# Splitting the weights of a hybrid attention block a load at a time (1,024 columns) in place of half a load

## The chip, the cores and the metric

One core of a Trainium2 chip runs the whole program. The metric is the device time of one execution in microseconds; of each kernel several executions are timed and the median is given. The profile is that of one further execution, taken by the hardware profiler.

The engines that matter: PE multiplies matrices (PEld loads its stationary operand), DVE and ACT do elementwise work, SP issues the transfers from memory (DMA). Every engine works through its own list of instructions in order and waits at one whose inputs are not ready.

## What is computed

A decoder block: a norm, one wide projection, two token mixers (sparse attention with a compressed, a selected and a sliding branch, and retention), gates, an output projection, a second norm and the residual. Cut to what matters here:

```python
h = rms_norm(x, norm_pre)                       # x: 512 tokens x 1024
proj = h @ w_in                                 # 1024 x 6936
q_n, k_c, v_c, k_s, v_s, k_w, v_w, g_n, z_n, q_r, k_r, v_r, z_r, m_a, m_b = split(proj)
kc = gelu(blocks(rope(k_c)) @ cmp_w1_k) @ cmp_w2_k        # compressed keys, values alike
o_a = g_0 * attend(q, kc, vc) + g_1 * attend(q, selected) + g_2 * attend(q, window)
y_a = (o_a * silu(z_n)) @ w_nsa_o
y_b = (group_norm(retention(q_r, k_r, v_r)) * silu(z_r)) @ w_ret_o
merged = sigmoid(m_a) * y_a + sigmoid(m_b) * y_b
y = x + rms_norm(merged @ w_out, norm_post)
```

## The kernel before

**Two halves of a number.** The matmuls take operands rounded to a shorter format (fp32r). To keep the precision of float32 each operand is split into its rounded value `hi` and the rest `lo`, and a product is three matmuls: hi by hi, hi by lo, lo by hi (`mm3`). For the weights this is done on the chip, while they stream in: a rounding (raw to `whi`, on ACT or DVE) and a subtraction (raw less `whi` to `wlo`, always on DVE).

**The weight stream.** All weights come in one order as 128-row pieces of 1024 columns, 512 KB each (`stream_shape`): load 0 in two halves, three more for the first projection, four of 560 columns (C, the keys' and values' columns), four for the queries (Q), eight for the hidden layer of the compression (H0 to H7), then blocks of four loads in the order of `PLAN` (Z, MA, ZR, QK, VR, ...; NO has two), and eight for the last projection. One load holds two *parts*: two k-tiles (128 rows of the contraction) of 512 columns each, and a matmul uses one part. In the hidden layer each part serves two steps of 256 columns, so a load is four pairs of matmuls.

**The buffers.** Raw loads lie in `NR` = 4 buffers (tile `raw`). `splitter` makes the parts in stream order. Each part takes one `whi` and one `wlo` tile of 512 columns, out of `NW` = 9 of each; the parts of C have storage of their own (`WC`). `in_ring` counts the parts without those of C. A tile comes free when the last matmul on its part has run (`used_up`, the list `done`). `split_lo` makes the subtraction; with the second part of a load it issues the next transfer (`load_next`, L315), so a raw buffer is filled again only once both its parts are split.

**The matmuls of a block.** `nat` (tokens as rows) and `tra` (transposed) run over the k-tiles for one output tile; four output tiles go through the same eight parts, and on the last of them each part is released as it is used. Then the next block's parts are wanted in the same order. `hidden` does the compression's first layer, H0 to H3 for the keys and H4 to H7 for the values.

**What sets the order.** The program is a set of generators. `Order` runs them while the kernel is built: it keeps a modelled time for PE (`now`) and for the other engines (`eng`), and always lets that generator go on which is ready by the model, by priority. `cp_any` puts a rounding on ACT or on DVE, whichever the model has done sooner (DVE has 400 ns against it). The subtraction of part p has priority 0 when p is at most `SOON` = 2 past the part that PE last asked for (`rank`), and 4 otherwise. The main line of projections has the lowest priority, 9, and attention 2 or 3. So each engine's list is fixed when the program is built, and a change of a duration or of a buffer count moves instructions on every engine.

Lines that the profile names: L222 matmul, L226 transpose on PE, L189 any ACT instruction, L197 rounding on DVE, L201 any two-input DVE instruction, L522 doubling of the keys ahead of their transposes, L315 the raw transfers. From L353 on, line numbers of the changed kernel are one higher.

## Time and profile before

| | |
|---|---|
| median of 3 executions | 528.35 us (528.35, 528.35, 529.0) |
| profiled execution, first to last instruction (span) | 527.0 us |
| granted clock of PE | 0.999 |
| PE busy | 518.6 us |
| DVE busy | 376.9 us |
| ACT busy | 272.8 us |
| DMA, mean over the span | 105 GB/s, 55.19 MB |

The profile gives for the profiled execution its span only; the time of an execution as a whole stands 1.35 us above it in the median. In its lines a group has line, engine, operation, output<-inputs by the names of their tiles (`bank` is a PSUM bank, `arena_r` and `arena_f` are large buffers cut up by hand), partitions x columns, and then busy time, mean ns of one, idle time of the engine just before and what ended it. In a timeline the columns are start, duration, engine, line, operation; "x3" is a run of three counted together, with the duration from the first start to the last end. A matmul's duration is longer than its distance to the next one, since they are pipelined.

### The profile page before, as it was taken

How to read it: one execution, taken by the hardware profiler on the slowest of the kernel's cores; microseconds unless marked ns; L12 is line 12 of the kernel's file. 1: busy time of each engine (PE TensorE's matmuls, PEld its weight loads, DVE VectorE, ACT ScalarE, POOL GpSimd, SP SyncE). 2: the span in 40 equal slices, each digit the busy share in tenths (PEclk: the TensorE clock that was granted, in tenths of full speed). 3: DMA queues.
4: the chain of work that ended last, by engine and by line, in shares of the span. 5: the costliest groups of instructions: out<-in, count | busy, mean ns of one | idle time of the engine just before them, and what ended most of it. 6: DMA issues, size and time to landing. Idle time of an engine off the chain costs nothing.

```text
span 527.0 us, 7380 instructions
## 1 busy us (share of the span) xinstructions
PE 518.6 (98%) x2634; PEld 437.5 (83%) x2634; DVE 376.9 (72%) x921; ACT 272.8 (52%) x592; POOL 12.6 (2%) x32
## 2 busy tenths in 40 slices
PE   9999999999999999999999999999999999999995
PEld 7888788888888888888888888888888888888885
DVE  6699799889879999887886576777637335345533
ACT  6664698687657888574535253625304324123411
POOL 1000000000000000000000000000000000000000
PEclk9999999999999999999999999999999999999999
DMA  8951027502204004133131341131905134304032
GB/s 320 370 183 41 21 81 214 186 2 90 71 1 137 24 5 156 40 106 114 41 120 44 137 157 44 48 115 40 326 34 159 33 127 138 104 1 159 1 99 100
DMA packets 18133, 55.19 MB, mean 105 GB/s; under 512 B 1969, under 2 KB 3249, under 8 KB 18097
## 3 DMA queue, kind: packets, MB, share of 16 engines
q1 hardware_dynamic: 17952, 54.60, 31.0%
q8 instruction: 20, 0.33, 0.3%
q14 instruction: 17, 0.13, 0.1%
q10 hardware_dynamic: 144, 0.14, 0.1%
HBM read 52.63 MB, written 2.10 MB: 104 GB/s over the span
## 4 chain that ended last, share of the span: by engine, by line
PE 89%; DVE 4%; DMA 4%; issue 2%; ACT 1%; SPq 0%; POOLq 0%; DVEq 0%; POOL 0%
PE bank L222 82%; PE bank L226 6%; DMA raw<-in_stream_dram 4%; DVE wlo L201 1%; DVE arena_r L201 0%; DVE arena_f L801 0%; ACT arena_f L189 0%; DVE arena_f L210 0%; DVE whi L197 0%; DVE arena_f L201 0%; SPq L435 0%; DVE arena_f L214 0%; SPq L315 0%; DVE stat L218 0%; ACT whi L189 0%
## 5 line engine op out<-in xcount | busy, mean ns | idle before, releaser
L189 ACT ACTIVATE whi<-raw 128x512 fp32r<-128x512 f32 x148 | 88.5, 626 | 50.7 <-PE bank L222 43.6
L201 DVE TENSOR_TENSOR wlo<-raw,whi 128x512 fp32r<-128x512 f32 x160 | 103.6, 684 | 5.7 <-ACT whi L189 4.2
L222 PE MATMUL bank<-whi,hTh 128*128 128x512 f32 x256 | 100.4, 408 | 0.2 <-ACT hTh L189 0.2
L222 PE MATMUL bank<-whi,hTl 128*128 128x512 f32 x256 | 96.5, 392 | 0.0
L222 PE MATMUL bank<-wlo,hTh 128*128 128x512 f32 x256 | 96.1, 391 | 0.0
L222 PE MATMUL bank<-arena_r 128*128 128x256 f32 (+2 forms) x328 | 69.9, 335 | 0.0
L222 PE MATMUL bank<-hTh,whi 128*128 128x512 f32 x160 | 63.8, 399 | 0.0
L222 PE MATMUL bank<-hTh,wlo 128*128 128x512 f32 x160 | 62.5, 390 | 0.0
L222 PE MATMUL bank<-hTl,whi 128*128 128x512 f32 x160 | 62.4, 390 | 0.0
L189 ACT ACTIVATE arena_f<-arena_f,stat 128x512 f32<-128x512 f32 (+3 forms) x106 | 56.8, 560 | 6.2 <-DVE stat L218 2.8
L222 PE MATMUL bank<-arena_r,whi 128*128 128x512 f32 x192 | 59.1, 389 | 0.0
L189 ACT ACTIVATE arena_r<-bank 128x512 fp32r<-128x512 f32 (+2 forms) x80 | 44.6, 569 | 25.8 <-PE bank L226 25.5
L201 DVE TENSOR_TENSOR arena_r<-bank,arena_r 128x512 fp32r<-128x512 f32 (+2 forms) x72 | 46.6, 655 | 15.0 <-ACT arena_r L189 14.5
L222 PEld LDWEIGHTS bank<-whi,hTl 128*128 128x128 f32 x256 | 48.4, 189 | 10.8
L222 PEld LDWEIGHTS bank<-arena_r 128*128 128x128 f32 x328 | 51.6, 189 | 6.9 <-DVE arena_r L201 0.4
L222 PEld LDWEIGHTS bank<-whi,hTh 128*128 128x128 f32 x256 | 48.5, 190 | 8.8 <-ACT hTh L189 0.5
L222 PEld LDWEIGHTS bank<-wlo,hTh 128*128 128x128 f32 x256 | 48.3, 189 | 8.2
L222 PE MATMUL bank<-whi,arena_r 128*128 128x512 f32 (+1 forms) x176 | 49.2, 353 | 0.0
L222 PEld LDWEIGHTS bank<-arena_r,whi 128*128 128x128 f32 x192 | 36.0, 188 | 7.6 <-DVE sg L214 0.2
L226 PE MATMUL bank<-ident,arena_f 128*128 128x128 f32 (+1 forms) x244 | 36.7, 273 | 1.0 <-DVE arena_f L522 1.0
L222 PE MATMUL bank<-arena_r,wlo 128*128 128x512 f32 x96 | 37.4, 389 | 0.0
L222 PEld LDWEIGHTS bank<-whi,arena_r 128*128 128x128 f32 x176 | 32.1, 189 | 4.5
(125 smaller groups left out, 656.2 us busy)
## 6 DMA issues: line engine op xcount, KB each, us to landing
raw<-in_stream_dram SPq DMA_DIRECT2D x79, 512.0 KB, 4.1
arena_f<-in_x_dram SPq DMA_DIRECT2D x8, 512.0 KB, 7.0
arena_f<-in_rope_r_dram SPq DMA_DIRECT2D x8, 256.0 KB, 2.7
arena_f<-in_xT_dram SPq DMA_DIRECT2D x7, 256.0 KB, 5.9
out_dram<-arena_f SPq DMA_DIRECT2D x6, 256.0 KB, 2.1
raw<-in_stream_dram SPq DMA_DIRECT2D x4, 280.0 KB, 7.5
raw<-in_stream_dram SPq DMA_DIRECT2D x2, 256.0 KB, 3.2
arena_f<-in_norm_post_dram SPq DMA_DIRECT2D x1, 512.0 KB, 7.5
```

Source lines behind the costliest of these rows:

```text
L189: S.activation(o, i, func, **kw)
L201: (V if e == "dve" else G).tensor_tensor(o, a, b, op=op)
L222: T.matmul(ps, a, b, start=start, stop=stop)
L226: T.transpose(ps, a, idn)
```

## The change

A load is split as a whole. `NW` goes from 9 tiles of 512 columns to 4 of 1024, of `whi` and of `wlo` each. One rounding and one subtraction cover both parts of a load; `split_lo` then enters two parts, which are the two halves of the wide tile, with one time. The splitter may begin a load when there is room for both its parts. The loads of C get storage of 560 columns in place of two of 280. Load 0, which arrives in two transfers, is still split in two halves (`ks` = 2).

```diff
-NR, NW = 4, 9
+NR, NW = 4, 4
...
-    WC = [tuple(at(44, 4480, FR)[:, (2 * p + i) * 280:(2 * p + i + 1) * 280] for i in range(2)) for p in range(KD)]
+    WC = [tuple(at(44, 4480, FR)[:, (2 * i + s) * 560:(2 * i + s + 1) * 560] for s in range(2)) for i in range(KD // 2)]
...
-            n = sum(pieces)
-            for k in range(2):
-                p = 2 * i + k
-                own = KD <= p < 2 * KD
-                yield lambda: own or in_ring(p) < in_ring(len(done)) + NW
...
+            n, p = sum(pieces), 2 * i
+            own = KD <= p < 2 * KD
+            yield lambda: own or in_ring(p + 1) < in_ring(len(done)) + 2 * NW
...
+                hi = wp.tile([P, 1024], FR, name="whi", tag="whi", bufs=NW)
+                lo = wp.tile([P, 1024], FR, name="wlo", tag="wlo", bufs=NW)
+            ks = 2 if i == 0 else 1
+            for k in range(ks):
                 r = max(raws[i][1], done[-1] if done and not own else 0.0)
                 yield r, "act"
...
+                c = slice(k * n // ks, (k + 1) * n // ks)
+                src, vh, vl = raws[i][0][:, c], hi[:, c], lo[:, c]
...
-                od.spawn(split_lo(p, hi, lo, src, vh, vl, e), rank(p))
-                nxt[0] = p + 1
+                od.spawn(split_lo(p + k, src, vh, vl, 2 // ks, e), rank(p + k))
+                nxt[0] = p + k + 2 // ks
                 yield
...
-        parts.append((hi, lo, r))
-        if p % 2 and len(raws) <= p // 2 + NR:
+        n = vh.shape[-1] // m
+        for j in range(m):
+            parts.append((vh[:, j * n:(j + 1) * n], vl[:, j * n:(j + 1) * n], r))
+        if len(parts) % 2 == 0 and len(raws) <= len(parts) // 2 - 1 + NR:
             load_next()
```

**How instructions move.** The matmuls and transposes are the same set; DVE has 726 rows (runs of like instructions counted once) in place of 754, ACT 355 in place of 376. Three places:

*The first keys' transposes, PE, while the loads of C are used.* `bank_88` is a transpose bank, the matmuls of 280 columns are the projections of C. The difference between the two lists, before marked "-" and after "+":

```order
 L222 MATMUL bank_84<-arena_r,hTh 128x280 x2
 L222 MATMUL bank_84<-arena_r,hTl 128x280
+L222 MATMUL bank_85<-arena_r,hTh 128x280 x2
+L222 MATMUL bank_85<-arena_r,hTl 128x280
 L226 MATMUL bank_88<-ident,arena_f 128x128 x2
 L222 MATMUL bank_85<-arena_r,hTh 128x280 x2
```

Three matmuls of the second token tile now stand ahead of the transposes of the first keys.

*The hidden layer.* DVE before, from the last scaling of an attention tile on (numbers name the tiles: `wlo_876`, `wlo_885` are the two halves of H1, `wlo_906` and `wlo_910` those of H2; `nat2` is a query tile in its rotary steps):

```order
L210 TENSOR_SCALAR arena_f_82<-arena_f_82,stat_828,gate_121 128x512
L197 CAST whi_875<-raw_375 128x512
L201 TENSOR_TENSOR wlo_876<-raw_375,whi_875 128x512
L197 CAST whi_884<-raw_375 128x512
L201 TENSOR_TENSOR arena_f_82<-nat2_109,cst_116 128x128
L201 TENSOR_TENSOR arena_f_82<-nat2_109,cst_116 128x8x8 x2
L201 TENSOR_TENSOR nat2_109<-arena_f_82 128x8x16
L201 TENSOR_TENSOR wlo_885<-raw_375,whi_884 128x512
L201 TENSOR_TENSOR arena_r_83<-bank5_89,arena_r_83 128x512
L201 TENSOR_TENSOR arena_r_83<-nat2_109,arena_r_83 128x8x64
L201 TENSOR_TENSOR wlo_906<-raw_385,whi_905 128x512
L201 TENSOR_TENSOR wlo_910<-raw_385,whi_909 128x512
```

DVE after, from the last scaling on (`wlo_797` is H1, `wlo_846` H2, `wlo_875` H3; in both lists the subtractions of H0 stand ahead):

```order
L210 TENSOR_SCALAR arena_f_82<-arena_f_82,stat_776,gate_121 128x512
L197 CAST whi_796<-raw_342 128x1024
L201 TENSOR_TENSOR wlo_797<-raw_342,whi_796 128x1024
L218 RECIPROCAL stat_781<-stat_781 128x1
L201 TENSOR_TENSOR stat_781<-stat_781,gate_121 128x1
L201 TENSOR_TENSOR arena_f_82<-nat2_109,cst_116 128x128
L201 TENSOR_TENSOR arena_f_82<-nat2_109,cst_116 128x8x8 x2
L201 TENSOR_TENSOR nat2_109<-arena_f_82 128x8x16
L197 CAST whi_845<-raw_356 128x1024
L197 CAST whi_874<-raw_526 128x1024
L201 TENSOR_TENSOR wlo_846<-raw_356,whi_845 128x1024
L201 TENSOR_TENSOR wlo_875<-raw_526,whi_874 128x1024
```

The roundings of H2 and H3, which stood on ACT, are on DVE now, both ahead of the subtraction of H2.

PE at the same place, before, around the second half of H1 and the first of H2:

```order
L222 MATMUL bank0_84<-wlo_876,arena_r_83 128x256
L226 MATMUL bank4_88<-ident_94,arena_f_82 128x128 x4
L222 MATMUL bank0_84<-whi_884,arena_r_83 128x256
L222 MATMUL bank0_84<-wlo_885,arena_r_83 128x256
...
L222 MATMUL bank6_90<-arena_r_83 128x512 x2
L226 MATMUL bank5_89<-ident_94,arena_f_82 128x128 x4
L222 MATMUL bank0_84<-whi_905,arena_r_83 128x256
```

PE after, from H0's first pair (`whi_762`, `wlo_763`) to H1's:

```order
L222 MATMUL bank0_84<-whi_762,arena_r_83 128x256
L222 MATMUL bank0_84<-wlo_763,arena_r_83 128x256
L222 MATMUL bank6_90<-arena_r_83 128x512 x2
L226 MATMUL bank4_88<-identr_99,arena_r_83 128x128 x4
L226 MATMUL bank5_89<-ident_94,arena_f_82 128x128 x4
...
L226 MATMUL bank4_88<-ident_94,arena_f_82 128x128 x4
L222 MATMUL bank0_84<-whi_796,arena_r_83 128x256
L222 MATMUL bank0_84<-wlo_797,arena_r_83 128x256
```

The attention matmuls and transposes that stood between the loads now stand ahead of H1's first pair; behind it come the other pairs of H1 and all of H2 and H3 with nothing between.

*The start of block ZR.* DVE before, from the evacuation of MA's last tile on (`sg`):

```order
L201 TENSOR_TENSOR sg_114<-bank_85,rsrow 128x512
L218 RECIPROCAL stat<-stat 128x1
L201 TENSOR_TENSOR stat<-stat,gate 128x1
L801 ISA arena_f,stat<-bank_86,maskp 128x384
L801 ISA stat 128x1
L201 TENSOR_TENSOR wlo<-raw,whi 128x512 x3
L201 TENSOR_TENSOR arena_r<-bank_88,arena_r 32x512
L201 TENSOR_TENSOR wlo<-raw,whi 128x512 x4
```

and after:

```order
L201 TENSOR_TENSOR sg_114<-bank_85,rsrow 128x512
L218 RECIPROCAL stat<-stat 128x1
L210 TENSOR_SCALAR arena_f<-arena_f,stat,gate 128x384
L802 ISA arena_f,stat<-bank_86,maskp 128x256
L802 ISA stat 128x1
...
L201 TENSOR_TENSOR wlo<-raw,whi 128x1024 x2
...
L802 ISA arena_f,stat<-bank_87,maskp 128x256
L802 ISA stat 128x1
...
L201 TENSOR_TENSOR wlo<-raw,whi 128x1024
```

The subtractions of loads two and three stand together behind two masked attention steps, that of load four behind two more; the first load's is far ahead in the list.

More of the change, by code (lines that the diff above doesn't have):

```diff
@@ L331, in splitter @@
         for i, (_, pieces) in enumerate(loads):
-            n = sum(pieces)
-            for k in range(2):
-                p = 2 * i + k
-                own = KD <= p < 2 * KD
-                yield lambda: own or in_ring(p) < in_ring(len(done)) + NW
-                while len(raws) <= i:
-                    yield lambda: len(raws) > i or len(raws) < NR or len(parts) > 2 * (len(raws) - NR) + 1
-                    if len(raws) <= i:
-                        load_next()
+            n, p = sum(pieces), 2 * i
+            own = KD <= p < 2 * KD
+            yield lambda: own or in_ring(p + 1) < in_ring(len(done)) + 2 * NW
+            while len(raws) <= i:
+                yield lambda: len(raws) > i or len(raws) < NR or len(parts) > 2 * (len(raws) - NR) + 1
+                if len(raws) <= i:
+                    load_next()
+            if own:
+                hi, lo = WC[i - KD // 2]
+            else:
+                hi = wp.tile([P, 1024], FR, name="whi", tag="whi", bufs=NW)
+                lo = wp.tile([P, 1024], FR, name="wlo", tag="wlo", bufs=NW)
+            ks = 2 if i == 0 else 1
+            for k in range(ks):
                 r = max(raws[i][1], done[-1] if done and not own else 0.0)
                 yield r, "act"
-                m = n // 2
-                src = raws[i][0][:, k * m:(k + 1) * m]
-                if own:
-                    hi, lo = WC[p - KD]
-                else:
-                    hi = wp.tile([P, 512], FR, name="whi", tag="whi", bufs=NW)
-                    lo = wp.tile([P, 512], FR, name="wlo", tag="wlo", bufs=NW)
-                vh, vl = hi[:, :m], lo[:, :m]
-                if p:
+                c = slice(k * n // ks, (k + 1) * n // ks)
+                src, vh, vl = raws[i][0][:, c], hi[:, c], lo[:, c]
+                if p + k:
                     e = cp_any(vh, src, r)
@@ L355, in splitter, with split_lo @@
                     e = od.op("dve", copy_ns(vh, src), r, True)
-                od.spawn(split_lo(p, hi, lo, src, vh, vl, e), rank(p))
-                nxt[0] = p + 1
+                od.spawn(split_lo(p + k, src, vh, vl, 2 // ks, e), rank(p + k))
+                nxt[0] = p + k + 2 // ks
                 yield
-    def split_lo(p, hi, lo, src, vh, vl, r):
+    def split_lo(p, src, vh, vl, m, r):
         yield lambda: rank(p)() == 0 or od.eng["dve"] <= od.now + SLACK
```

## The prediction

> **What bounds the kernel now.** I read the page from the top: busy times, slices, chain.
>
> ```profile
> PE 518.6 (98%) x2634; PEld 437.5 (83%) x2634; DVE 376.9 (72%) x921; ACT 272.8 (52%) x592; POOL 12.6 (2%) x32
> ...
> PE   9999999999999999999999999999999999999995
> ...
> DVE  6699799889879999887886576777637335345533
> ACT  6664698687657888574535253625304324123411
> ...
> PE bank L222 82%; PE bank L226 6%; DMA raw<-in_stream_dram 4%; DVE wlo L201 1%; DVE arena_r L201 0%; DVE arena_f L801 0%; ACT arena_f L189 0%; DVE arena_f L210 0%; DVE whi L197 0%; DVE arena_f L201 0%; SPq L435 0%; DVE arena_f L214 0%; SPq L315 0%; DVE stat L218 0%; ACT whi L189 0%
> ```
>
> The matrix engine (PE) is busy in every slice but the last, and its matmuls are 88% of the chain that ended last. DVE and ACT, whose instructions the change merges, have idle time over the whole span; wlo has 1% of the chain. So the sum of their time decides nothing. What can move the span is how often PE waits, and that I read from the waits of PE and from windows of 10 us (columns: stretch, busy us and records of PE, weight load, DVE, ACT, POOL).
>
> ```profile
> PE bank L1277 <- DVE rsrow L239: 1.0, 1, 1.0
> PE bank L226 <- DVE arena_f L522: 1.0, 1, 1.0
> PE bank L222 <- ACT hTh L189: 0.2, 1, 0.2
> ...
> 30.00:40.00 10.00, 8.99 (x72) 8.77 (x71) 9.47 (x46) 6.42 (x22) 0.47 (x2) 1.00 0.39 140
> ...
> 70.00:80.00 10.00, 9.86 (x66) 8.29 (x65) 9.32 (x26) 9.76 (x21) 0.00 (x0) 1.00 0.35 113
> ...
> 160.00:170.00 10.00, 10.00 (x49) 8.40 (x48) 9.51 (x26) 6.82 (x17) 0.00 (x0) 1.00 0.48 142
> ```
>
> Only three named waits, 2.2 us of 527. The first and third are the cold start. The second, near 31 us, is the wait for the rotated keys. PE also loses a little at 70 to 80 us, where DVE and ACT are nearly full: the hidden layer of the compression. At 160 to 170 us, where one block of weights follows another, DVE is as full (9.51) and yet PE does not wait. These are the three places where the change can act.
>
> **What merging saves.** By kind of instruction (count, busy us and mean ns):
>
> ```profile
> L201 DVE TENSOR_TENSOR wlo<-raw,whi 128x512 fp32r<-128x512 f32 x160 | 103.6, 684 | 5.7 <-ACT whi L189 4.2 <-PE bank L226 1.0
> L201 DVE TENSOR_TENSOR arena_r<-arena_f,arena_r 128x1024 fp32r<-128x1024 f32 x2 | 2.4, 1215 | 0.0
> L189 ACT ACTIVATE arena_f<-arena_f 128x1024 f32<-128x1024 f32 x4 | 4.2, 1062 | 2.1 <-DMA arena_f<-in_x_dram 2.1
> L197 DVE CAST whi<-raw 128x512 fp32r<-128x512 f32 x11 | 4.6, 423 | 1.1 <-PE bank L222 0.7 <-DMA raw<-in_stream_dram 0.3
> ```
> ```profile
> 77.06 1.28 DVE L201 TENSOR_TENSOR wlo<-raw,whi 128x512 fp32r<-128x512 f32 x2
> ```
>
> The profile has subtractions of 1024 columns of the same types: 1.215 us. Two of 512 back to back take 1.28, so a load saves about 0.07 us of DVE: 79 merged loads x 0.07 = 5.5 us of 376.9. A rounding of 1024 on DVE: a copy of 768 columns takes 0.56 us (at 31.16 below), (560 - 423) / 256 = 0.54 ns a column more than one of 512, so 423 + 512 x 0.54 = 700 ns, an estimate; 0.65 from start to start. On ACT the row of 1062 ns stands against 1.14 us for two of 512 in the timeline below: 0.08 us a load, some 6 us of 272.8. None of it is on the chain: PE's work hides it, and the matmuls are the same set. I count it as nothing by itself; if that cover went, it would be worth up to the 1% that wlo has in the chain.
>
> [...]
>
> **What merging costs: latency.** A matmul on the first half of a load now waits for the whole load. From free tile to usable pair it was 0.6 (half of that 1.14) + 0.68 = 1.3 us and becomes 1.06 + 1.22 = 2.3. A tile also comes free only when its second half has been used, and the ninth tile is gone: 18 tiles of 512 columns (9 of each kind) become 8 of 1024. At a change of block, in the last pass over a block of eight k-tiles, each k-tile is three matmuls of 0.227 us (start to start below), 0.68. Before, half j takes the tile that half j - 1 left: 8 steps from free to wanted, 5.4 us. Now load i takes the tile of load i: freed after half 2i + 1, wanted 6 steps later, 4.1 us. The reserve falls from 5.4 - 1.3 = 4.1 us to 4.1 - 2.3 = 1.8, by 2.3 us, less whatever the engines' queues add.
>
> **1. The keys at 31 us.**
>
> ```profile
> 30.18 0.29 PE L222 MATMUL bank<-arena_r,hTl 128*128 128x280 f32 x1
> ...
> 30.57 0.29 PE L222 MATMUL bank<-arena_r,hTl 128*128 128x280 f32 x1
> ...
> 31.16 0.56 DVE L522 COPY arena_f<-nat 128x768 f32<-128x768 f32 x1
> ...
> 31.86 0.41 PE L226 MATMUL bank<-ident,arena_f 128*128 128x128 f32 x2 [1.01 <-DVE arena_f L522]
> ```
>
> PE stands from 30.57 + 0.13 to 31.86: 1.17 us lost. The order now puts three more matmuls of 280 columns ahead of that transpose: 30.57 - 30.18, 0.39 us of cover. On DVE three wide subtractions replace two roundings and six halves ahead of the copy, but the last of them still waits for the same landing and now for a whole rounding, so I leave the copy's end within 0.1 us of before. Gain **0.3**; bounds a loss of 0.2 (the copy later by a half subtraction, 0.6, with 0.39 of cover) and a gain of 1.17 (all of it).
>
> **2. The hidden layer, 73 to 91 us.** Loads H0 to H7, four pairs of matmuls of 256 columns each.
>
> ```profile
> 72.40 0.16 DVE L218 RECIPROCAL stat<-stat 128x1 f32<-128x1 f32 x1
> ...
> 73.07 0.42 DVE L197 CAST whi<-raw 128x512 fp32r<-128x512 f32 x1
> 73.36 0.46 PE L226 MATMUL bank<-identr,arena_r 128*128 128x128 f32 x4
> ...
> 73.66 0.35 PE L222 MATMUL bank<-whi,arena_r 128*128 128x256 f32 x1
> ...
> 74.46 0.56 DVE L201 TENSOR_TENSOR arena_f<-nat,cst 128x128 f32<-128x128 f32 x3
> ```
> ```profile
> 75.26 0.68 DVE L201 TENSOR_TENSOR wlo<-raw,whi 128x512 fp32r<-128x512 f32 x1
> 75.28 0.66 PE L226 MATMUL bank<-ident,arena_f 128*128 128x128 f32 x4
> ...
> 75.69 0.36 PE L222 MATMUL bank<-whi,arena_r 128*128 128x256 f32 x1
> ...
> 75.97 1.14 ACT L189 ACTIVATE whi<-raw 128x512 fp32r<-128x512 f32 x2
> 76.00 0.39 PE L222 MATMUL bank<-wlo,arena_r 128*128 128x256 f32 x1
> ...
> 77.30 0.36 PE L222 MATMUL bank<-whi,arena_r 128*128 128x256 f32 x1
> ...
> 77.80 0.38 PE L222 MATMUL bank<-wlo,arena_r 128*128 128x256 f32 x1
> 78.03 0.28 PE L222 MATMUL bank<-whi,arena_r 128*128 128x256 f32 x1
> 78.14 0.28 PE L222 MATMUL bank<-wlo,arena_r 128*128 128x256 f32 x1
> ```
>
> A pair's second matmul starts 0.115 us after its first (78.03 to 78.14). At 75.69 it took 0.31, at 77.30 it took 0.50: 0.2 + 0.4 = 0.6 us of stall, each time PE starting 0.06 us after the subtraction ended (75.94, 77.74). Halves are used the moment they are made.
>
> Now DVE's order has, behind the subtraction of H1, the four rotary rows, then two whole roundings (H2, H3) and only then the subtraction of H2. From 73.07, when the last scaling before is done: a subtraction from a bank that was behind and now stands ahead (0.60) and the second half of H0 (0.6) push back, a reciprocal and scaling that are gone pull forward (73.07 - 72.40, 0.7): 73.6. Rounding of H1 0.65, subtraction 1.2: 75.4. Reciprocal and product 0.35, the four rotary rows 0.8 (74.46 to 75.26): 76.6. Two roundings 1.3: 77.9; subtraction of H2 1.2: **79.1**. PE: H0's first matmul came at 73.66; a group of transposes that stood before it now stands behind (75.28 to 75.69, 0.4), so 73.3. From there to H2's subtraction lie two matmuls of 512 (0.45), three groups of transposes (0.3 at 73.36, twice 0.4), eight pairs (1.84) and one matmul more: 3.5 us. PE wants H2 at **76.8**, with nothing between H1 and H3 to fill in. Stall 2.3 us. H3's subtraction ends 1.2 later where PE takes 0.9 for H2: 0.3. H4 is behind two more subtractions of 0.6 and its own 1.2, 82.4, where PE with the transposes and attention matmuls between would be at 82.0: 0.4. Raw loads are issued when a subtraction frees their buffer: H4's after H0's, at about 72, and by this row it lands at 76, when ACT can take it.
>
> ```profile
> raw<-in_stream_dram SPq DMA_DIRECT2D x79, 512.0 KB, 4.1
> ```
>
> So the transfers do not add here. Sum 3.0 against 0.6 before: 2.4. DVE reaches this stage with some of the 0.07 us a load in hand and could be earlier by up to 0.5; I take **+1.8**; bounds -0.6 (DVE comes free 2 us sooner than I read, and both stalls go) and +3 (none of that 0.5, and H5 late too).
>
> **3. Changes of block, 125 to 270 us.** The nearest one in reserve, the start of block ZR at 164 us:
>
> ```profile
> 163.94 1.89 DVE L201 TENSOR_TENSOR wlo<-raw,whi 128x512 fp32r<-128x512 f32 x3
> ...
> 165.52 0.40 PE L222 MATMUL bank<-wlo,hTh 128*128 128x512 f32 x1
> 165.75 0.40 PE L222 MATMUL bank<-whi,hTl 128*128 128x512 f32 x1
> ...
> 166.57 2.50 DVE L201 TENSOR_TENSOR wlo<-raw,whi 128x512 fp32r<-128x512 f32 x4
> ...
> 167.84 0.40 PE L222 MATMUL bank<-wlo,hTh 128*128 128x512 f32 x1
> ```
>
> The first of the three ended near 164.6 (0.60 each), and PE used it at 165.52: 0.9 us of reserve; the first of the four near 167.2, used at 167.84: 0.6. The full 2.3 us of coarseness less 0.6 to 0.9 would be a stall of some 1.5 us. Against it, the order now holds attention matmuls between the last pass and this one, and has the first load's two halves done long before. There I find DVE late by about 0.4 us at the second load. Of the five tight changes (MA, ZR, QK, VR, ZR) I take that one in full and the rest as covered: **+0.5**; bounds 0 (PE has no wait there now, so there is nothing to gain) and 5 x 1.5 = 7.5. After 290 us DVE is 30 to 50% busy and the reserve of 1.8 us stands: 0.
>
> **Sum.** -0.3 + 1.8 + 0.5 = +2.0 us on the span of 527.0, so 529.0. Outside the span lie 528.35 - 527.0 = 1.35 us, taking the profiled execution for one at the median of the three runs, of which two agree. 530.35: I say **530.3 us**, 0.4% slower.
>
> **Rivals.** *No change*: the hidden layer costs only what PE can't fill, about 1 us, the keys give back 0.3 to 1.1, the changes of block are covered: 528.35 + 1.0 - 0.7 = 528.7. For it: PE had no wait at any change of block; against it: the reserve of 0.06 us in the hidden layer. *Faster*: the fixed cost saved brings DVE forward before 31 and 73 us, and both stalls go: -1.2 - 0.6 = -1.8, 526.6. For it: 9.32 to 9.51 us of DVE in 10 there, so that every 0.07 us counts; against it: the stalls hang on a latency that is longer now. *Much slower*: four coarse tiles at each of the tight changes of block. It decides from where the wait for the whole load exceeds the 0.6 to 0.9 us of reserve plus the attention work moved between; at 0.5 to 0.8 us a change, the five add 2.5 to 4 us in place of 0.5: 529.85 + 3.25 = 533.1. That the change doesn't do what it says is excluded: the order has 79 wide subtractions in place of 158.
>
> **How the numbers follow.** The forecast (529.2 to 531.5) 0.42, no change 0.25, faster 0.16, much slower 0.17. A measurement here tells about 0.2% (1.06 us) from no change. A little of the forecast (0.04) lies below 529.4, so faster 0.16, same 0.29, slower 0.55. The range 526.8 to 533.2 leaves out about half of the faster case and half of the much slower one, 0.16.
>
> **What would show it.** Right: PE waits named for wlo near 77 to 83 us, of 1.5 to 3 us in sum, one of them near 2, DVE's two roundings ahead of them; the wait for L522 at 31 us down to about 0.9; PE with short waits on wlo near 165 us and none after 290. Wrong: no PE wait in 73 to 91 us (then ACT or an earlier free tile gave the roundings sooner), a longer wait at 31 us, or PE records thinned out at each change of block, which would be the much slower case. The mean durations should be 1.2 us for wlo, 1.06 for a rounding on ACT, 0.70 on DVE; if they are shorter, case two or three gains.

## The result and the profile after

| | before | after |
|---|---|---|
| median of 8 executions each, same chip | 528.75 us (528.35 to 532.93) | 532.64 us (532.24 to 534.78) |
| ratio, 95% interval | | 1.0061 [1.0041, 1.0081] |
| profiled execution, span | 527.0 us | 533.0 us |
| granted clock of PE | 0.999 | 0.995 |
| PE, DVE, ACT busy | 518.6, 376.9, 272.8 us | 520.4, 370.6, 263.8 us |

The changed kernel is slower by 0.6%, by the ratio 3.2 us (the medians differ by 3.9). The executions of either kernel lie in two groups (spans of 530.4 to 531.0 and of 531.8 to 534.4 us over 13 executions of the changed kernel, 526.5 to 527.9 and 528.3 to 531.0 over 62 of the kernel before), and the profile after fell in the longer group, the one before in the shorter: so the 6.0 us between the two profiles are not the change's alone. Between the shorter groups lie 4.0 us in this series (medians 532.41 and 528.42) and 3.3 us in a later one (532.46 and 529.13).

The page of the changed kernel, the lines that answer to those of before:

```profile
PE 520.4 (98%) x2634; PEld 437.9 (82%) x2634; DVE 370.6 (70%) x832; ACT 263.8 (50%) x520; POOL 12.6 (2%) x32
...
PE   8979998999999999999999999999999999999995
...
PEclk9989999999999999999999999999999999999999
...
PE bank L222 75%; PE bank L226 6%; DMA raw<-in_stream_dram 4%; DVE wlo L201 3%; DVE arena_r L201 1%; DMA arena_f<-in_xT_dram 1%; DVE arena_f L201 1%; ACT whi L189 1%; ACT arena_f L189 1%; DVE arena_f L802 1%; DVE arena_f L210 0%; DVE nat L201 0%; DVE whi L197 0%; DVE arena_f L214 0%; ACT arena_r L189 0%
```

DVE and ACT have 6.3 and 9.0 us less to do, as the sum of the merged instructions said. The end comes later all the same: the PE row has 8s and a 7 at its start where it was all 9s, PEclk has an 8 in the third slice (27 to 40 us), and `wlo` rose from 1% of the chain to 3%. The waits of PE (line, what for, us in all, times, longest) say which:

```profile
PE bank L226 <- DVE arena_f L523: 2.7, 1, 2.7
PE bank L222 <- DVE wlo L201: 2.2, 4, 1.4
PE bank L1278 <- DVE rsrow L239: 1.0, 1, 1.0
PE bank L222 <- ACT hTh L189: 0.3, 1, 0.3
PE bank L222 <- DVE arena_r L201: 0.2, 1, 0.2
```

The wait for the doubled keys (L522 before, L523 now) grew from 1.0 to 2.7 us, and four waits for `wlo` are new. Named waits leave out part of the loss, so I also worked out from the records of all matmuls what PE lost in each stretch: for every matmul the distance from its start to the next start, less the median distance of that form (source line and shape) in the kernel before. The sums differ by 5.95 us between the two profiles, which is the 6.0 of the spans. All kernels of this study by that measure, in us (stretches in us of the span; "tile" is the unit in which a `whi` or `wlo` buffer is taken and given back, "instr." the columns of a rounding or subtraction):

| kernel | tile, instr. | start 0-20 | keys 20-42 | hidden layer 66-100 | changes of block 125-285 | all |
|---|---|---|---|---|---|---|
| before | 512, 512 | 1.82 | 1.29 | 1.69 | 2.26 | 8.38 |
| after | 1024, 1024 | 1.14 | 4.49 | 2.80 | 4.57 | 14.33 |
| after, again (exp. 12) | 1024, 1024 | 1.02 | 3.71 | 2.53 | 4.55 | 13.09 |
| 1: before, 8 tiles | 512, 512 | 1.73 | 2.00 | 1.51 | 2.58 | 9.22 |
| 2: after, halves | 1024, 512 | 0.99 | 4.01 | 3.65 | 3.65 | 14.06 |
| 3: after, H on ACT | 1024, 1024 | 1.72 | 3.82 | 2.69 | 3.63 | 13.10 |
| 4: after, keys first | 1024, 1024 | 1.55 | 0.22 | 3.77 | 4.46 | 11.56 |
| 5: 4 with five whi tiles | 1024, 1024 | 0.91 | 0.85 | 3.83 | 2.76 | 10.55 |
| 6: before, keys first | 512, 512 | 1.25 | 0.63 | 1.89 | 2.79 | 7.84 |
| 7: 4 with SOON = 4 | 1024, 1024 | 1.16 | 0.74 | 3.42 | 2.44 | 11.95 |
| 8: 4 with halves | 1024, 512 | 3.66 | 0.11 | 3.72 | 3.57 | 12.71 |
| 9: 5, halves in H | 1024, mixed | 1.12 | 0.54 | 3.77 | 2.67 | 10.25 |
| 10: before, 8 tiles, keys first | 512, 512 | 0.90 | 0.50 | 1.52 | 2.60 | 6.73 |
| 11: before, keys at load 8 | 512, 512 | 3.43 | 0.07 | 1.91 | 2.78 | 9.23 |

Between before and after: start -0.68, keys +3.20, hidden layer +1.11, changes of block +2.31, everything else 0. The same kernel twice (after, and again) differs by 0.3 us or less in the last two columns. A changed order of the lists moves them by more, even where an edit does not aim at them: the hidden layer lost 1.0 us more in experiment 4, the changes of block 0.9 less in experiment 3. So a single difference of up to 1 us between two kernels decides nothing; a column that agrees over several kernels does.

**The keys.** Timeline of the changed kernel (start, duration, engine, line, operation):

```profile
29.21 1.06 ACT L189 ACTIVATE whi<-raw 128x1024 fp32r<-128x1024 f32 x1 [0.56 <-DMA raw<-in_stream_dram]
...
29.91 0.29 PE L222 MATMUL bank<-arena_r,hTl 128*128 128x280 f32 x1
...
30.31 1.23 DVE L201 TENSOR_TENSOR wlo<-raw,whi 128x1024 fp32r<-128x1024 f32 x1 [0.39 <-ACT whi L189]
...
32.17 0.56 DVE L523 COPY arena_f<-nat 128x768 f32<-128x768 f32 x1
...
32.87 0.66 PE L226 MATMUL bank<-ident,arena_f 128*128 128x128 f32 x2 [2.67 <-DVE arena_f L523]
```

and windows of 2 us (stretch, busy us and records of PE, PEld, DVE, ACT, POOL, then PEclk, DMA share, GB/s):

```profile
30.00:32.00 2.00, 0.20 (x2) 0.00 (x0) 1.66 (x5) 2.00 (x5) 0.00 (x0) 1.00 0.82 293
32.00:34.00 2.00, 1.13 (x5) 1.16 (x6) 1.90 (x9) 2.00 (x8) 0.00 (x0) 0.71 0.86 293
34.00:36.00 2.00, 2.00 (x11) 1.99 (x10) 1.92 (x12) 0.76 (x3) 0.32 (x1) 0.50 0.52 195
36.00:38.00 2.00, 2.00 (x17) 2.00 (x16) 1.26 (x8) 0.96 (x5) 0.00 (x0) 0.93 0.00 0
```

The chain runs from a landing (of Q's third load, at 29.11 us) over a rounding on ACT to a subtraction on DVE, in whose queue the keys' steps and their copy stand behind that subtraction. PE comes 0.66 us sooner than before (29.91 against 30.57; its start cost less) and is released 1.0 later. Then a second loss follows that no wait names: the granted clock was 0.50 from 32.85 to 36.26 us, and 11 matmuls ran from 34 to 36 us where 18 ran at 1.00 in experiments 1 and 4. Of the 3.20 us, 2.67 - 1.01 = 1.66 are the longer wait; the other 1.54, what is left of the difference, go with the low clock.

**The hidden layer**, from H0's first matmul on:

```profile
75.98 0.28 PE L222 MATMUL bank<-whi,arena_r 128*128 128x256 f32 x1
76.04 0.69 DVE L197 CAST whi<-raw 128x1024 fp32r<-128x1024 f32 x1
...
76.76 1.22 DVE L201 TENSOR_TENSOR wlo<-raw,whi 128x1024 fp32r<-128x1024 f32 x1
...
78.97 1.29 DVE L197 CAST whi<-raw 128x1024 fp32r<-128x1024 f32 x2
...
79.72 0.38 PE L222 MATMUL bank<-whi,arena_r 128*128 128x256 f32 x1
...
80.18 2.35 DVE L201 TENSOR_TENSOR wlo<-raw,whi 128x1024 fp32r<-128x1024 f32 x2
...
81.45 0.38 PE L222 MATMUL bank<-wlo,arena_r 128*128 128x256 f32 x1 [1.35 <-DVE wlo L201]
```

Two whole roundings (H2, H3, from 78.97) stand ahead of the subtraction of H2. PE's pair on H2 took 81.45 - 79.72 = 1.73 us where 0.115 is usual: 1.62 us lost at one place.

**The changes of block.** The start of ZR at 174 us, and of the second ZR at 273 us:

```profile
173.46 2.36 DVE L201 TENSOR_TENSOR wlo<-raw,whi 128x1024 fp32r<-128x1024 f32 x2
...
174.16 0.40 PE L222 MATMUL bank<-whi,hTh 128*128 128x512 f32 x1
...
174.73 0.50 PE L222 MATMUL bank<-wlo,hTh 128*128 128x512 f32 x1 [0.18 <-DVE wlo L201]
...
272.33 0.39 PE L222 MATMUL bank<-whi,hTh 128*128 128x512 f32 x1
...
273.11 0.50 PE L222 MATMUL bank<-wlo,hTh 128*128 128x512 f32 x1 [0.40 <-DVE wlo L201]
```

At 0.227 us from start to start these pairs lost 0.34 and 0.55; one in VR at 244 us lost 0.41. Each time `whi` is there and `wlo` is not. The remaining 1.0 us is in smaller pieces over all of these changes, among them 0.1 us behind each late pair and, at 146 us, 0.35 where 0.16 was lost before, ahead of a matmul of attention.

### The profile page after: what moved, and what is told of

Read it like the earlier page. It is cut to its first block, busy times and chain, and to the rows that moved or that the text cites. A ratio compares the mean times of both kernels' runs of the same rounds, so it can differ in the third digit from the quotient of the medians.

```text
span 533.0 us, 7183 instructions
## 1 busy us (share of the span) xinstructions
PE 520.4 (98%) x2634; PEld 437.9 (82%) x2634; DVE 370.6 (70%) x832; ACT 263.8 (50%) x520; POOL 12.6 (2%) x32
## 4 chain that ended last, share of the span: by engine, by line
PE 81%; DVE 9%; DMA 5%; issue 3%; ACT 2%; SPq 0%; POOLq 0%; DVEq 0%; POOL 0%; ACTq 0%
PE bank L222 75%; PE bank L226 6%; DMA raw<-in_stream_dram 4%; DVE wlo L201 3%; DVE arena_r L201 1%; DMA arena_f<-in_xT_dram 1%; DVE arena_f L201 1%; ACT whi L189 1%; ACT arena_f L189 1%; DVE arena_f L802 1%; DVE arena_f L210 0%; DVE nat L201 0%; DVE whi L197 0%; DVE arena_f L214 0%; ACT arena_r L189 0%
## 5 line engine op out<-in xcount | busy, mean ns | idle before, releaser
L201 DVE TENSOR_TENSOR wlo<-raw,whi 128x1024 fp32r<-128x1024 f32 (+1 forms) x81 | 96.3, 1207 | 10.6 <-ACT whi L189 9.9
L189 ACT ACTIVATE whi<-raw 128x1024 fp32r<-128x1024 f32 (+1 forms) x72 | 75.3, 1052 | 46.2 <-PE bank L222 39.8
L189 ACT ACTIVATE arena_f<-arena_f,stat 128x512 f32<-128x512 f32 (+3 forms) x113 | 59.4, 556 | 3.0 <-DVE stat L218 1.5
L222 PEld LDWEIGHTS bank<-whi,hTl 128*128 128x128 f32 x256 | 48.0, 188 | 10.4
L226 PEld LDWEIGHTS bank<-ident,arena_f 128*128 128x128 f32 (+1 forms) x244 | 29.6, 140 | 9.7 <-issue 2.9
```

The lines of the kernel that those rows point to most:

```text
L189: S.activation(o, i, func, **kw)
L201: (V if e == "dve" else G).tensor_tensor(o, a, b, op=op)
L222: T.matmul(ps, a, b, start=start, stop=stop)
L226: T.transpose(ps, a, idn)
```

## The experiments

Two theories stood at the outset: that the *width* of the merged instructions costs the time (a consumer waits for the whole load), and that the *lost ninth tile* does. A third formed after the second experiment: that the *unit of the ring* does, since a buffer of 1024 columns is taken and given back as one, whatever the instructions' width.

### 1. The kernel before with eight tiles

```diff
-NR, NW = 4, 9
+NR, NW = 4, 8
```

> The kernel before with 8 tiles of 512 columns of each kind in place of 9, the storage that the changed kernel has, and still one rounding and one subtraction for each half. Theory A (the loss comes from waiting for whole loads and from tiles that come free two halves at a time): next to nothing is lost, span within 0.6 us of 527.0, the wait for the doubled keys near 31 us stays about 1.0 us, waits on wlo sum to under 0.6 us. Rival B (the ninth tile is what the changed kernel lacks): most of the loss is here already, 530 us or more by the span, with waits on wlo of over 1.5 us at the hidden layer and at the changes of block.

529.34 us against 529.28; ratio 0.9998 [0.9978, 1.0018]. The same storage as the changed kernel's, in halves, loses nothing in the hidden layer (1.51 against 1.69 us) and 0.3 at the changes of block. The wait for the keys was 1.7 us, not the 1.0 expected, and the profiled span 527.9; the time shows no loss. The lost ninth tile is not the cause.

### 2. The changed kernel with its instructions halved

```diff
-            ks = 2 if i == 0 else 1
+            ks = 2
```

> The changed kernel with its 4 wide tiles, but every load (those of C too) rounded and subtracted in two halves, each usable when it is made. Theory A: the waits on wlo at the hidden layer and at the changes of block fall from 2.2 us to under 0.6, the wait for the doubled keys from 2.7 to about 1.0; span 527.5 to 528.5. Rival B (storage that comes free in units of 1024): the waits stay, span 530 or more. Rival C (the merged instructions save engine time that counts): slower than the changed kernel.

533.49 us; ratio 1.0073 [1.0049, 1.0098]. Every rounding and subtraction is 512 columns wide again, in tiles of 1024, and none of the time came back. Waits of PE in this kernel:

```profile
PE bank L226 <- DVE arena_f L523: 2.2, 1, 2.2
...
PE bank L226 <- ACT arena_r L189: 0.9, 1, 0.9
PE bank L222 <- DVE wlo L201: 0.8, 2, 0.5
PE bank L222 <- DVE arena_r L201: 0.7, 2, 0.4
```

The waits for `wlo` shrank from 2.2 to 0.8 us, but the hidden layer as a stretch lost 3.65, more than with wide instructions; the changes of block lost 3.65 in place of 4.57. The width of the instructions is not the cause by itself; it names the wait, and without it another name stands there.

### 3. The hidden layer's roundings on ACT

```diff
-                    e = cp_any(vh, src, r)
+                    e = act(vh, src, r=r) if 12 <= i < 20 else cp_any(vh, src, r)
```

> The changed kernel with the roundings of H0 to H7 all on ACT. Theory A (the two roundings on DVE ahead of the subtraction of H2 make the stall at 79.7 us): that wait of 1.4 us falls under 0.6 us; DVE has 3 roundings fewer; span 0.8 to 1.4 us less than the changed kernel's, the wait at 31 us untouched. Rival (ACT is as full there, 8.5 of 10 us, and its queue is in order): the roundings come behind attention work and the wait stays between 1 and 2 us, only with ACT's rounding as its start.

533.49 us; ratio 1.0074 [1.0048, 1.0100]. The stall at H2 fell from 1.62 to 0.94, and others of 0.25, 0.27 and 0.54 came behind it: the stretch lost 2.69 in place of 2.80. The two roundings ahead of the subtraction, which the prediction read off the order, are how the lateness shows, not where it comes from.

### 4. The keys' steps first

The splitter does not begin load 9 until the first keys are doubled, so their steps stand ahead of that load's subtraction in DVE's queue. In `splitter`, and behind the doubling of the keys:

```diff
             n, p = sum(pieces), 2 * i
+            if i == 9:
+                yield od.need("kd0")
...
         e = doubled(kn, 0, 384, kd, e)
+        od.flags.add(f"kd{t}")
```

> The changed kernel with the second and later loads of Q held back until the first keys are doubled, so that ACT evacuates the keys ahead of the wide roundings and DVE doubles them ahead of the wide subtractions. Theory A (in ACT's and DVE's order the whole rounding and subtraction of Q's third load, and the transfer it waits for, stand ahead of the keys): the wait for the doubled keys falls from 2.7 to under 0.6 us, the granted clock stays 1.00 from 30 to 40 us, span 528 to 529 and 2 to 4 us under the changed kernel. Rival (the loads of C landed 1.4 us late in the profiled execution, by chance): the wait is about as long as before, 1.0 us, in any order, and the time gains under 0.5 us.

531.97 us; ratio 1.0053 [1.0035, 1.0072]; span 530.2. Windows of this kernel:

```profile
30.00:32.00 2.00, 2.00 (x18) 2.00 (x17) 1.90 (x11) 2.00 (x4) 0.00 (x0) 1.00 0.56 207
32.00:34.00 2.00, 2.00 (x18) 2.00 (x17) 1.97 (x5) 1.45 (x7) 0.48 (x1) 1.00 0.02 8
34.00:36.00 2.00, 2.00 (x18) 2.00 (x17) 1.93 (x10) 0.90 (x3) 0.28 (x1) 1.00 0.27 53
```

The wait is gone and the clock stays at 1.00; the stretch lost 0.22 in place of 4.49. That is 4.3 us in the profile, of which only 2.8 arrive in the span, since the hidden layer lost 1.0 more (why, was not tested), the start 0.4 and the stretch from 42 to 66 us 0.3. The four executions (spans 530.1 to 531.0) lie where the changed kernel's shorter ones do: against those it gains 0.5 us by the medians. The wait went as theory A says, and the time gained what the rival says. So the keys are a large part of the profiled difference and a small part of the change's cost.

### 6. The same in the kernel before

> The kernel before (halves, nine tiles) with Q's second and later loads held back until the first keys are doubled. Theory A (the wait for the doubled keys, and the executions 1.5 to 2 us longer than the others, come from the order on ACT and DVE at 27 to 32 us): wait under 0.3 us, span 525.8 to 526.4, every execution within 0.6 us of the fastest: about 1 us faster than before, and faster than both kernels. Rival (Q's loads, split later, then miss their own turn, or the order of the rest of the program gets worse by chance): span 527 or more.

528.04 us against 529.45; ratio 0.9973 [0.9956, 0.9991]: faster than both kernels. The keys' wait was there before the change, and taking it away is worth 1.4 us by the medians. The wait fell to 0.4 us, not under 0.3, and the executions still differ by 2.0 us (spans of 525.9 to 527.9), which theory A had within 0.6.

### 5, 7. What gives the changes of block back

Experiment 5 is experiment 4 with five wide `whi` tiles; `wlo` has four, taken only when the subtraction is made.

```diff
-NR, NW = 4, 4
+NR, NW, NL = 4, 5, 4
...
-                lo = wp.tile([P, 1024], FR, name="wlo", tag="wlo", bufs=NW)
+                lo = None
...
+        if lo is None:
+            yield lambda: in_ring(p + m - 1) < in_ring(len(done)) + 2 * NL
+            if p != 1:
+                low[0] = wp.tile([P, 1024], FR, name="wlo", tag="wlo", bufs=NL)
```

> The changed kernel with the keys first (as in the run before it) and five wide tiles for the rounded halves, four for the rest: the next block's first rounding can be made while the last pass still holds the other four. Theory A (a wide tile comes free so late that rounding, 1.05 us, and subtraction, 1.2 us, no longer fit before it is wanted): with the rounding of one load out of the way the lost time of PE falls, from 3.8 to about 2.5 us between 66 and 100 us and from 4.5 to about 3 between 125 and 285; span 528 to 529.3. Rival (the subtraction, which still waits for its own tile and for DVE, is what comes last): the waits on wlo stay near 2.1 us and the span within 0.6 of 530.1.

530.47 us; ratio 1.0010 [0.9991, 1.0029]. The changes of block lost 2.76 in place of 4.46: with one wide rounding more in reserve they are back at what half tiles give. The hidden layer stayed at 3.83, with one wait of PE for `wlo` of 1.4 us; but in this profile the clock fell behind that wait (below), and 1.3 of the 3.83 us were lost while it was low.

Experiment 7 is experiment 4 with `SOON = 4`, which puts the next subtractions ahead of attention's work earlier.

> The changed kernel with the keys first, and the subtraction of a load given first priority up to four parts ahead of PE in place of two: two wide loads, as two halves were one load ahead before. Theory A' (the order of DVE was made for halves; subtractions stand too late in it): waits on wlo fall from 2.1 to under 1 us, span 528.5 to 529.5. Rival (the tile comes free too late, whatever the order): waits on wlo stay near 2 us, span 529.7 to 531.

532.45 us; ratio 1.0053 [1.0034, 1.0073]. The changes of block lost 2.44, with no wait for `wlo` there any more (the 1.6 us that are left lie in the hidden layer). But PE now waits 1.3 us for a row of attention (`rsrow`, at 51 us), and 335 to 380 us lost 1.41 in place of 0.42: the gain is given back elsewhere. So at the changes of block the wide tile by itself does not force the loss: with the same four tiles of 1024 columns, refilled as a whole, another order of DVE's list takes it away there, at a price in other places.

### 8, 10. The unit of the ring by itself

Experiment 8 is experiment 4 with `ks = 2`: tiles of 1024, instructions of 512. Experiment 10 is experiment 6 with `NW = 8`: the same storage and instructions of the same width, in tiles of 512. Both have the keys first.

> The changed kernel with the keys first, four wide tiles, and every load rounded and subtracted in two halves. Theory A'' (what costs is that a tile is filled again only when both its halves are used, not that a matmul waits for the whole load): span within 0.7 us of the 530.1 of the same kernel with whole loads. Rival (the longer latency of the merged instructions costs): span within 0.7 us of 527.4, that of 8 single tiles.

> Halves in 8 single tiles, keys first: the storage of the kernel with four wide tiles, keys first, filled again half by half. Theory A'' (the unit in which a tile comes free carries the loss that is left after the keys): span 526.0 to 527.0, lost time of PE under 2 us between 66 and 100 us and under 3 between 125 and 285, against 3.7 and 3.6 with halves in wide tiles and 3.8 and 4.5 with whole loads. Rival (the ninth tile matters once the keys no longer hide it): span 527.5 or more.

Tiles of 1024: 531.40 us; ratio 1.0041 [1.0022, 1.0059]. Tiles of 512: 527.53 us; ratio 0.9964 [0.9951, 0.9978], the fastest of all kernels here. Without the start, which varies from run to run (below), PE lost 12.71 - 3.66 = 9.05 us in the one and 6.73 - 0.90 = 5.83 in the other, and 11.56 - 1.55 = 10.01 in experiment 4. Of the 4.2 us between the changed kernel and half tiles, both with the keys first, halving the instructions gives 1.0 back and halving the unit 3.2, of which 2.2 lie in the hidden layer. At the changes of block the kernels without the hold say the same: halving the instructions gave 0.9 us in both pairs (the changed kernel to 2, 4 to 8), halving the unit 1.1 and 1.0 more (2 to 1, 8 to 10). So there width and unit each carry about half of the loss, in the hidden layer the unit alone. Timeline of experiment 8 about H0's first matmul:

```profile
69.51 1.14 ACT L189 ACTIVATE whi<-raw 128x512 fp32r<-128x512 f32 x2
...
70.30 0.39 PE L222 MATMUL bank<-whi,hTl 128*128 128x512 f32 x1
...
76.17 0.35 PE L222 MATMUL bank<-whi,arena_r 128*128 128x256 f32 x1
...
77.07 0.62 ACT L189 ACTIVATE whi<-raw 128x512 fp32r<-128x512 f32 x1
```

and of experiment 10:

```profile
65.39 0.62 ACT L189 ACTIVATE whi<-raw 128x512 fp32r<-128x512 f32 x1
...
67.05 0.61 ACT L189 ACTIVATE whi<-raw 128x512 fp32r<-128x512 f32 x1
...
68.98 0.62 ACT L189 ACTIVATE whi<-raw 128x512 fp32r<-128x512 f32 x1
...
71.30 0.62 ACT L189 ACTIVATE whi<-raw 128x512 fp32r<-128x512 f32 x1
...
72.47 0.36 PE L222 MATMUL bank<-whi,arena_r 128*128 128x256 f32 x1
```

With half tiles a rounding follows each part of the last pass over Q, about every 2 us, and H0 and H1 (four halves) are rounded by 71.9, before PE begins on H0. With whole tiles in experiment 8 only H0 is; the first rounding of H1 begins 0.9 us after PE has started on H0, and stands then in the same queue as the tail of attention. In the changed kernel it was the same (H1's rounding at 76.04, PE's start at 75.98); in the kernel before, half of H1 came ahead (73.07 against 73.66).

It is not the tile itself that comes last there. In experiment 8 the matmul at 70.30 is the last on the load whose tile H1 takes, and by the transfers' records H1's raw load had landed at 45.04; from about 70.7 to 77.07 only the order of ACT's list, with attention's work ahead, kept the rounding back. Nor is H1 always the place. In experiments 4, 5, 7 and 9 it is rounded before PE begins on H0, and the loss stands at a later load, in experiment 4 at H3 (rounded from 75.67 on, where PE was ready for it at about 76.16 and got its second matmul at 78.10):

```profile
75.67 1.99 ACT L189 ACTIVATE whi<-raw 128x1024 fp32r<-128x1024 f32 x2
...
76.76 0.39 PE L222 MATMUL bank<-whi,arena_r 128*128 128x256 f32 x1 [0.45 <-ACT whi L189]
78.10 0.39 PE L222 MATMUL bank<-wlo,arena_r 128*128 128x256 f32 x1 [0.95 <-DVE wlo L201]
```

What holds over all kernels is the sum, in the table's column for the hidden layer: with half tiles it lost 1.5 to 1.9 us, with whole ones 2.5 to 3.8, whatever the instructions' width, their engine or the fifth `whi` tile. That the unit carries the loss is shown so; by which path is argued: a rounding can be entered in its engine's list only when the build's model has the tile given back, a wide tile is given back later, and the rounding then stands behind more of attention's work. No run changes that place in the list alone.

### 9. Halves in the hidden layer, on five whi tiles

Experiment 5 with `ks = 2` for loads 12 to 23 as well.

> Five wide tiles for the rounded halves and four for the rest, keys first, and the loads of the hidden layer and of Z rounded and subtracted in halves, all others whole. Theory L (in the hidden layer the merged pair's latency of 2.3 us comes last): lost time of PE between 66 and 100 us falls from 3.8 to about 2, span 526.3 to 527.3, as good as the halves. Theory U (in the hidden layer too it is the wide tile that comes free late, whatever the instructions' width): 3 to 4 us stay, span 528 to 529.

531.00 us; ratio 1.0025 [1.0002, 1.0047]. The hidden layer lost 3.77, with no fall of the clock in that stretch of its profile, as much as experiment 4 with neither. A fifth `whi` tile and narrow instructions together do not help there; `wlo` still came free in whole loads.

### 11, 12. An earlier hold, and the changed kernel again

> The kernel before with all four loads of Q held back until the first keys are doubled, one load more than in the run that was faster than before. If the order on ACT and DVE is what the keys wait for: the last 0.4 us of that wait go, span 525.5 to 526.1, 0.2 to 0.5 us under that run. Rival (Q's first load then comes late, or the rest of the order gets worse): 526.3 or more.

Experiment 6 with the hold at load 8 in place of 9: 528.85 us; ratio 0.9986 [0.9971, 1.0001]. The keys' stretch lost 0.07 in place of 0.63, but the profile has 3.43 us lost at the start; as a time it is not better than experiment 6, and the span of 527.9 is the rival's.

> The changed kernel unaltered, a second profile. Theory M (its executions come in two groups, spans of 530.4 to 531.0 and 532.3 to 533.0 us, by when the third load of C lands and whether the clock then falls): with that load landing by 23.2 us the wait for the doubled keys is 1.0 to 2.0 us, the granted clock stays 1.00 from 32 to 38 us and the span is near 530.6; with it landing after 23.7, the wait is 2.3 us or more, the clock falls to half and the span is near 532.6. Rival (the groups have another cause, such as the clock at the start): landing and wait do not go together so.

The changed kernel once more: 533.54 us; ratio 1.0079 [1.0042, 1.0117]. Hidden layer and changes of block repeat (2.53 and 4.55). The wait for the keys is 1.9 us in place of 2.7. By the transfers' records the third load of C landed at 23.54 us, not 24.23, and the keys' copy ended at 31.86, not 32.73; so the end follows the landing, by 8.3 and 8.5 us. In the kernels with half tiles it follows by more, 8.9 (before: 22.85 to 31.72) and 9.4 (experiment 1: 22.99 to 32.37). Between the two lies the transfer of Q's third load, which is issued into the raw buffer that the third load of C leaves, and for which the rounding at 29.21 waits. It takes 3.4 and 3.2 us in the two profiles of the changed kernel, 3.8 and 4.2 in the two with halves. Ahead of it merging takes 0.1 us off (issue 1.50 us behind the landing in place of 1.59 and 1.60), behind it 0.1 is added (3.62 us from the transfer's landing to the copy's end in place of 3.52). So merging did not lengthen this chain, and the landing of C is what varies most (22.46 to 24.23 over the kernels with merged tiles, 22.85 to 24.10 over those with halves). The landing lies between the two cases of theory M, and after a wait that the theory put with a full clock the clock fell again:

```profile
32.00:34.00 2.00, 2.00 (x11) 2.00 (x12) 1.90 (x12) 1.88 (x5) 0.04 (x1) 0.61 0.87 336
34.00:36.00 2.00, 2.00 (x11) 1.99 (x11) 1.79 (x11) 0.96 (x5) 0.27 (x1) 0.54 0.16 64
```

## Why the prediction was right or wrong

The direction was right (slower), and the measured 532.64 us lies in the range, 2.3 us above the forecast of 530.3. It lies above the stretch that the prediction gave to its own forecast (529.2 to 531.5), where the prediction had the *much slower* rival, with a chance of 0.17. And the sum came as near as it did in part by luck: the hidden layer was taken too high, the changes of block too low. Step by step:

- **What merging saves: right.** DVE and ACT have 6.3 and 9.0 us less busy time, where 5.5 and some 6 were worked out, and none of it shows in the span. By kind, in the changed kernel:

```profile
L201 DVE TENSOR_TENSOR wlo<-raw,whi 128x1024 fp32r<-128x1024 f32 x79 | 95.0, 1220 | 10.6 <-ACT whi L189 9.9
L189 ACT ACTIVATE whi<-raw 128x1024 fp32r<-128x1024 f32 x71 | 74.7, 1058 | 46.1 <-PE bank L222 39.8 <-DMA raw<-in_stream_dram 4.0 <-ACT whi L189 1.1
L197 DVE CAST whi<-raw 128x1024 fp32r<-128x1024 f32 x8 | 5.4, 689 | 0.8 <-PE bank L222 0.8
```

  1.220, 1.058 and 0.689 us against the forecast 1.2, 1.06 and 0.70. The *faster* rival, in which the time saved brings DVE forward and both stalls go, did not come.
- **1, the keys: wrong.** Forecast -0.3 us, and the profile has +3.20. The step that failed is the reading of the order: the three more matmuls of 280 columns stand ahead of a *later* group of keys' transposes, not of the first, which is what the section on the change says. Both lists have 24 matmuls of 280 columns ahead of the first group; it is the third group, at 38.95 us before and 41.92 after, that has 75 ahead of it in place of 72. There was no cover to gain. The size it reached in the profile comes from a later landing and from the clock, which the prediction did not have; experiment 12 and the chain's 8.3 to 8.5 us against 8.9 to 9.4 say that merging did not lengthen it. The landings of the two kinds of kernel overlap (experiment 12), so nothing here shows the change as the cause of the late one.
- **2, the hidden layer: the wait right, its size too large.** From H0's first matmul PE wanted H2's second matmul after 3.9 us (81.45 less the wait, 1.62, less 75.98; forecast 3.5), and the subtraction let it go on after 5.4 (forecast 5.8): a stall of 1.62 where 2.3 was forecast. The stretch cost +1.11 and +0.84 in the two profiles against the term of +1.8. The named wait near 77 to 83 us came as announced, with 1.35 us by its name. But the cause behind it was not the order of two roundings (experiment 3 took that away and gained 0.1 us); it is the unit in which tiles come free (8 against 10), by a path that stays open.
- **3, changes of block: mechanism right, term mis-sized.** +0.5 was taken, by charging one of five changes and calling the others covered; +2.31 and +2.29 were measured. The reserve was worked out as shrinking by 2.3 us, and then attention's matmuls between were trusted as cover. By the records each of the 40 subtractions at these five changes ended at least 0.34 us ahead of the first matmul on its part before; after, 5 of 20 ended behind it (by 0.07 to 0.73), one at each change. Three changes have a stall of 0.34 to 0.55, the rest is lost in smaller pieces. That was the *much slower* rival, whose 0.5 to 0.8 us a change is close to 2.3 / 5 = 0.46. Halved instructions give 0.9 us of it back and the halved unit 1.0; experiment 7 took the loss away by the order of DVE's list, experiment 5 by a fifth `whi` tile. Nothing after 290 us, as forecast, though DVE is busy there in the kernel before for 67% of 290 to 400 us and 46% of 400 to 500.
- **The sum.** Outside the span lie 1.8 us (528.85 with a span of 527.1 in a run of the kernel before), not 1.35: the median and the profiled execution were not the same execution. That is a slip in the time of before, too, and so does not touch the difference. Hidden layer and changes of block measured are 1.11 + 2.31 = 3.4 us, with nothing for the keys; the shorter executions differ by 3.3 and 4.0. Forecast was +2.0.

Why both kernels have a longer group of executions can be read in part from the clock on record for each. A profile in which the clock fell in mid-run has a mean granted clock of 0.994 to 0.996, one without a fall 0.997 to 0.999. Of the 62 executions of the kernel before, 38 have 0.997 or more, and all but one of these have spans of 526.5 to 527.9; 24 have 0.996 or less, and 22 of these have 528.3 to 531.0. In the changed kernel all six longer executions have 0.996 or less, and six of the seven shorter ones 0.998 or more. So the longer group goes along with a mean clock as low as that of the profiles in which the clock fell. The keys' wait is one source of it, since experiments 4, 7 and 10, which have the keys first, have spans within 1.3 us (5 and 6 within 1.6 and 2.0). In experiment 8, which has them first too, spans go from 528.8 to 531.5 with no low clock on record; its profile is of a long one and lost 3.66 us at the start (below). What stays open is why the third load of C lands when it does, since the changed kernel and experiment 4, whose edit acts only from Q's second load on, differ by 1.8 us, and by which path the coarse unit costs the hidden layer its time.

## What to carry to other kernels

A ring of buffers is worth what its unit of refill lets enter the lists early, not the bytes in it: the same storage in eight tiles of 512 columns or four of 1024 differed by 0.77% here (0.9964 against 1.0041, instructions of equal width; 0.6% by PE's lost time without the start), while merging instructions on engines that wait anyway gave nothing, and cost 0.9 us where loads hand over. When a change makes buffers coarser, charge every place where one set of buffers hands over to the next, and do not count other work between as cover unless its rows are shown to fill that gap. And look in the in-order queue for prefetch work that stands ahead of what the bounding engine waits for: holding back the splits of Q's second and later loads until the first keys were doubled made the kernel before 0.27 to 0.36% faster (experiments 6 and 10, the latter with eight tiles).

## What the hardware showed unexpectedly

**After waits of 1.4 to 2.7 us the granted clock fell to half in five profiles.** It fell to 0.5 for 3.41 us after PE's waits for the keys of 1.92 (experiment 12), 2.0 (experiment 3), 2.2 (experiment 2) and 2.67 us (the changed kernel), and not after 1.0 (before) or 1.7 (experiment 1, the first two rows below: the clock stays at 1.00). But it also fell in the hidden layer of experiment 5, after a wait of 1.41 (third row), and not there after waits of 1.35 (the changed kernel, both profiles) and 1.44 (experiment 9): the length of the wait alone does not decide it.

```profile
32.00:34.00 2.00, 1.50 (x12) 1.49 (x13) 1.93 (x10) 2.00 (x7) 0.00 (x0) 1.00 0.80 274
34.00:36.00 2.00, 2.00 (x18) 2.00 (x18) 1.83 (x13) 1.13 (x6) 0.29 (x1) 1.00 0.55 223
```

```profile
80.00:82.00 2.00, 2.00 (x9) 1.81 (x9) 2.00 (x5) 2.00 (x4) 0.00 (x0) 0.51 0.63 205
```

By the clock records in the traces each of the five falls lasted 3.41 us and began a whole number of times 3.413 us after the record of a full clock began (8 times in four of them, in the changed kernel from 5.54 to 32.85 us; 22 times in experiment 5). With each trace cut into stretches of that length from there on, PE was busy for 0.77 to 1.89 us in the stretch ahead of each fall; of all other stretches before the programs' last microseconds only one was as empty (1.68 us, experiment 1, at its wait for the keys).

Ahead of the falls PE stood idle for 1.4 to 2.7 us and was busy for the rest of the stretch. Why the clock fell there, and not in experiment 1, is not shown.

**The start varies by up to 2.8 us, with the time at which the clock record begins.** From 5 to 10 us experiment 8 ran 12 matmuls and the changed kernel 22; first experiment 8, then the changed kernel:

```profile
5.00:10.00 5.00, 4.91 (x12) 3.85 (x13) 3.51 (x6) 2.79 (x6) 0.00 (x0) 1.00 1.03 370
```

```profile
5.00:10.00 5.00, 5.00 (x22) 4.12 (x22) 3.72 (x7) 3.67 (x6) 0.00 (x0) 1.00 1.01 379
```

5.0 / 12 is 0.42 us a matmul in place of 0.23 (5.0 / 22), a factor of 1.8; from 10 to 15 us the two ran 23 and 24. Where the record has 0.50, 11 matmuls ran in 2 us in place of 18, a factor of 1.6 (the keys, above). Here the rows show 1.00, but the clock record of experiment 8 begins only at 10.42 us, with a full clock, and that of the changed kernel at 5.54; ahead of its first entry there is no record, and the view shows 1.00. That the clock was low there is the author's inference; no record shows it. The loss at the start goes with that time: 0.90 to 1.16 us in the seven profiles whose record begins at 4.8 to 5.8 us, 1.55 to 1.82 in the four at 6.5 to 7.0, 3.43 and 3.66 in the two at 10.0 and 10.4 (experiment 6, with 1.25 us and a record from 4.0 on, stands apart). Half and wide tiles lie among each other in this, so single profiles are better compared by stretch than by span.
